# Full-height lo tiles for the second logits matmul of a two-layer hybrid trunk on one Trainium2 core

## The chip, the cores and the metric

The kernel is one program on one core of one Trainium2 chip. Its time is the device time of one launch in microseconds, and of several runs the median is taken. Lower is better. The profile is one execution of the same program, recorded by the hardware profiler: for each engine every instruction with its start and its length.

The engines are named as in the profile: PE is the tensor engine's matmul, PEld its weight load (a matmul needs its stationary operand loaded first), DVE the vector engine, ACT the scalar engine, POOL the GpSimd engine, and SP the queue that issues the DMAs.

## The reference

The reference is an encoder trunk of two layers over 1024 tokens of width 1024. The first layer is a gated DeltaNet mixer, the second (FoX) a softmax attention with a forget gate. Each layer norms its input, mixes it, multiplies by a SiLU gate, projects back and adds to the residual stream. The change is in the attention of the second layer, with 16 heads of 64 elements each:

```
q = rmsnorm(q, qn_w) * 64 ** -0.5
k = rmsnorm(k, kn_w)
cum = cumsum(log_sigmoid(f + f_bias))          # per head, over the tokens
logits[t, s] = q_t . k_s + cum[t] - cum[s]     # for s <= t, else -inf
p = softmax(logits)
o = (p @ v) * silu(z)
y = o @ w_out
```

All of it is in float32. The kernel's products must be more exact than one pass of the tensor engine in its fast float32 form (fp32r) gives, and so operands are split into a hi part (rounded to fp32r) and a lo part (the rest), and products are summed from two or three passes.

## The kernel before, in words

Layer A (the DeltaNet) takes the first two thirds of the program, the FoX layer the rest. Both are written as Python generators, one for each stream of work. A class `Flow` (its functions `step`, `add`, `bank`, `free`) runs the generators by priority against a model of the tensor engine's time, and so writes out by hand the order of all PE instructions. The model prices a matmul by the number of columns that it streams, and for fp32r at least by the columns of its weights (`_cost`); the number of rows is not in it. The order on the other engines is left to the tile framework, which also puts in the waits for tiles and frees a tile's memory when its readers are done.

The FoX layer goes over eight groups `g` of two heads (`j` = 0, 1), and in each over two halves of 512 tokens (`hh`). The streams are:

- `in_proj` projects the tokens to q, k, v and z, three passes for each product (`mm3`). It supplies the matmuls named `mm` in the profile. It is the longest stream, and the others are placed between its matmuls.
- `post` (inside `in_proj`) transposes the normed q and k of one half into tile `tr` and makes the operands of the logits. For a head that lies in rows `own` (0 to 63 for j = 0, 64 to 127 for j = 1), tile `qs[:, j]` holds the hi part of the scaled q in both halves of its 128 rows (ACT, lines 1332 and 1333), tile `ks[:, j]` holds the hi part of k in rows `own` (ACT, line 1347) and its lo part in the other 64 (DVE, line 1348), and tile `ql` holds the lo part of q in rows `own` (DVE, line 1334). `ql` has one plane for both heads, since they lie in different rows.
- `logits` makes, for each of four row tiles of 128 queries (`tt`) and for each block of up to 512 keys (`b`), one PSUM bank `lg` with two or three matmuls: `qs` with all 128 rows of `ks` (hi times hi, plus hi times lo), then `ql` with the 64 rows `own` of `ks` (lo times hi), and in the block on the diagonal a small bf16 matmul of an identity with the mask. Two banks take turns. DVE adds the gate's sums, takes the row minimum (the logits are kept negated) and writes the block to SBUF (line 1422); ACT takes the exponential (line 1430).
- `values` transposes the probabilities (`pt`), splits them on ACT and DVE (`pth`, `ptl`, lines 1465 and 1466) and multiplies with v into `oT`; `fold_out` divides by the row sums and multiplies with the gate.
- After the last group `out_proj_b` projects back. For the last group (`g == NG - 1`) `fold_out` splits its result into `oh` and `ol` in SBUF; `oh` is taken from the ring of `ql` tiles.

For each head and half there are thus 4 row tiles with one block (first half) or two (second half): 16 heads x (4 + 8) = 192 blocks, each with one `ql` matmul. In the first half every block is on the diagonal; in the second half the first block of a row tile is not and has 512 columns.

The tiles of the FoX layer come from two pools. The one on the right side of SBUF is opened after layer A's output projection and lies over the memory of that layer; a tile in it waits for the last users of what lay there.

Of the kernel before, what the change touches and what calls it, by code (L numbers as in the profile page):

```python
# [12 lines left out]
ALU = mybir.AluOpType  # L13
# [81 lines left out]


class Flow:
    """Emits the pieces of several streams in the order in which the tensor engine shall run them."""

    def __init__(self, tc):  # L100
        self.tc = tc
# [70 lines left out]
def tile_trunk(  # L172
# [158 lines left out]
    def acc_bank():  # L331
        return flow.bank("mm", 2, lambda: pmm.tile([P, 512], F32, name="mm", tag="mm", bufs=2))

# [1 line left out]
    sx = ctx.enter_context(ExitStack())  # L335
    px = sx.enter_context(tc.tile_pool(name="px", bufs=1, side="right"))

# [774 lines left out]
            flow.step()  # L1112


# [1 line left out]
    with ExitStack() as sb:  # L1116
        pb = sb.enter_context(tc.tile_pool(name="pb", bufs=1, reuse_waits="tile"))
        psb = sb.enter_context(tc.tile_pool(name="psb", bufs=1, space=PS))
# [95 lines left out]
        fb = bt([P, 16], "fb")  # L1214
        nc.sync.dma_start(fb, f_bias.broadcast_to([P, 16]))
        cum_d = dram.tile([16, S], F32, name="cum_d", tag="cum_d")

        def forget():
            raw = bt([P, KT, 16], "wf_r")
# [55 lines left out]
        def in_proj(u):  # L1275
            g = u["g"]
            while len(bq) < KT:
                bload()
            ws = [bq.pop(0) for _ in range(KT)]
            for hh in range(2):  # L1280
                yield from hold(lambda: done["unit"] >= 4 * g - 4)
                kn = None
                u["v", hh] = v = bt([P, 4, 2, P], "v", 4, F32R)
                for tt in range(4):
                    t = hh * 4 + tt
                    tok = slice(t * P, (t + 1) * P)
                    yield from hold(lambda: done["n2"] > t)
                    ps = yield from acc_bank()
                    for k in range(KT):
                        hi, lo = ws[k]  # L1290
                        mm3(
                            ps[:, 0:384], h2_h[:, k, tok], h2_l[:, k, tok], hi[:, 0:384], lo[:, 0:384],
                            k == 0, k == KT - 1,
                        )
                        if k < KT - 1:
                            yield 0
                    if kn is None:
                        yield from hold(lambda: done["post"] == 2 * g + hh)
                        kn = bt([P, 4, 2 * P], "kn", 1)
                    sq = bt([P, 256], "sq", 1)  # L1300
                    nc.scalar.activation(sq, ps[:, 0:256], AF.Square)
                    ss = bt([P, 4], "ss", 2)
                    nc.vector.tensor_reduce(
                        ss, sq.rearrange("p (n f) -> p n f", f=64), axis=AX.X, op=ALU.add
                    )
                    nc.vector.tensor_scalar(ss, ss, 1.0 / 64, EPS, op0=ALU.mult, op1=ALU.add)  # L1306
                    rs = bt([P, 4], "rs", 2)
                    nc.gpsimd.tensor_tensor(rs, ss, mhalf[:, 0:4], op=ALU.pow)  # L1308
                    vv = ps[:, 256:384].rearrange("p (n f) -> p n f", f=64)
                    nc.scalar.copy(v[:, tt, :, 0:64], vv)  # L1310
                    nc.vector.tensor_tensor(
                        v[:, tt, :, 64:128], vv, v[:, tt, :, 0:64].bitcast(F32), op=ALU.subtract
                    )
                    nc.vector.tensor_tensor(
                        kn[:, tt].rearrange("p (n f) -> p n f", f=64),
                        ps[:, 0:256].rearrange("p (n f) -> p n f", f=64), bc(rs, 2, 64), op=ALU.mult,
                    )
                    flow.free(ps, R_IP)
                    yield 0

                def post(kn=kn, hh=hh):
                    yield from hold(lambda: done["lg"] >= 4 * g - 4 + 3 * hh)
                    yield Y_Q0
                    tr = yield from pst("tr", 1)
                    for tt in range(4):
                        tr_(tr[:, tt * P : (tt + 1) * P], kn[:, tt, 0:P], ident)
                    qs = bt([P, 2, 512], "qs", 3, F32R)
                    ql = bt([P, 512], "ql", 3, F32R)
                    for j in range(2):
                        own, oth = slice(64 * j, 64 * j + 64), slice(64 - 64 * j, 128 - 64 * j)  # L1330
                        sc = qk_c[own, 0:1]
                        nc.scalar.activation(qs[own, j], tr[own], AF.Copy, scale=sc)
                        nc.scalar.activation(qs[oth, j], tr[own], AF.Copy, scale=sc)
                        nc.vector.scalar_tensor_tensor(
                            ql[own], tr[own], sc, qs[own, j].bitcast(F32), op0=ALU.mult, op1=ALU.subtract
                        )
                    flow.free(tr, Y_TB)
                    u["q", hh] = (qs, ql)
                    yield Y_Q1
                    tr = yield from pst("tr", 1)  # L1340
                    for tt in range(4):
                        tr_(tr[:, tt * P : (tt + 1) * P], kn[:, tt, P : 2 * P], ident)
                    ks = bt([P, 2, 512], "ks", 4, F32R)
                    for j in range(2):
                        own, oth = slice(64 * j, 64 * j + 64), slice(64 - 64 * j, 128 - 64 * j)
                        sc = qk_c[own, 1:2]
                        nc.scalar.activation(ks[own, j], tr[own], AF.Copy, scale=sc)
                        nc.vector.scalar_tensor_tensor(
                            ks[oth, j], tr[own], sc, ks[own, j].bitcast(F32), op0=ALU.mult, op1=ALU.subtract
                        )  # L1350
                    flow.free(tr, Y_TB)
                    u["k", hh] = ks
                    done["post"] += 1
                    yield 0

                flow.add(post(), 3)
            zs = [None, None]
            for n in range(KT + ZL):
                for hh in range(2):
                    k = n - ZL * hh  # L1360
                    if not 0 <= k < KT:
                        continue
                    if zs[hh] is None:
                        zs[hh] = yield from acc_bank()
                    tok = slice(hh * HALF, hh * HALF + HALF)
                    hi, lo = (w[:, 384:512] for w in ws[k])
                    mm3(zs[hh], hi, lo, h2_h[:, k, tok], h2_l[:, k, tok], k == 0, k == KT - 1)
                    if hh:
                        bload()
                    if k < KT - 1:  # L1370
                        yield 0
                        continue
                    u["z", hh] = zg = bt([P, 512], "zg", 4)
                    th = bt([P, 512], "wraw", 2)
                    nc.scalar.activation(th, zs[hh], AF.Tanh, scale=0.5)
                    nc.vector.scalar_tensor_tensor(zg, th, 1.0, zs[hh], op0=ALU.add, op1=ALU.mult)
                    flow.free(zs[hh], R_Z)
                    yield 0
# [11 lines left out]
        def logits():  # L1390
            yield from hold(lambda: "fg" in done)
            last, cur = {}, None
            for n, (u, hh, j) in enumerate(units()):
# [3 lines left out]
                if cur != 2 * g + j:  # L1397
# [1 line left out]
                    cumb = bt([P, S], "cumb", 1)  # L1399
                    nc.sync.dma_start(cumb, cum_d[cur : cur + 1, :].broadcast_to([P, S]))  # L1400
                    yield 2500
                hp = slice(64 * j, 64 * j + 64)
                qa, ql = u["q", hh]
                sums = bt([P, 4], "sums", 3)
                pts = []
# [2 lines left out]
                for tt in range(4):  # L1408
# [4 lines left out]
                    for b in range(hh + 1):  # L1413
                        w = min(512, L - b * 512)
                        ka = u["k", b][:, j]
                        ps = yield from pst("lg", 2)
                        last_b = b == hh
                        mm(ps[:, 0:w], qa[:, j, qs], ka[:, 0:w], start=True, stop=False)
                        mm(ps[:, 0:w], ql[hp, qs], ka[hp, 0:w], start=False, stop=not last_b)
                        if last_b:  # L1420
                            mm(ps[:, w - P : w], identb, maskb, start=False, stop=True)
                        nc.vector.tensor_tensor_reduce(  # L1422
                            out=lg[:, b * 512 : b * 512 + w], in0=ps[:, 0:w],
                            in1=cumb[:, b * 512 : b * 512 + w], op0=ALU.add, op1=ALU.min,
                            scale=1.0, scalar=3.0e38 if b == 0 else mx[:, 0:1],
                            accum_out=mx[:, b : b + 1],
                        )
                        flow.free(ps, R_LG)
                        yield Y_G1
# [53 lines left out]
        def fold_out(u, hh, j, sums, og):  # L1483
# [13 lines left out]
                return  # L1497
            if g == NG - 1:
                nc.vector.tensor_tensor(og, og, u["z", hh], op=ALU.mult)
                oh, ol = bt([P, 512], "ql", 3, F32R), bt([P, 512], "zg", 4, F32R)  # L1500
                split(oh, ol, og, lo_eng=nc.vector)
                tail["o7", hh] = oh, ol
                tail["o7t", hh] = flow.t + Y_O7
# [221 lines left out]
```

## Time and profile before

| | before |
|---|---|
| median of 3 runs | 2207.39 us (2204.01 to 2208.75) |
| span of the profiled execution, first to last instruction | 2203.7 us |
| PE busy (matmul) | 1917.6 us, 87% |
| PEld busy (weight load) | 1541.6 us, 70% |
| DVE busy | 1587.4 us, 72% |
| ACT busy | 1048.1 us, 48% |
| POOL busy | 798.0 us, 36% |
| mean granted clock of the tensor engine | 0.940 |
| first and last `ql` matmul | 1478.1 and 2117.2 us |

The page of the profile lists no other time for the profiled execution than its span. A row of the timeline has the start in us, the length in us, the engine, the line, the operation, the tiles as out<-in, for PE the rows*columns of the weights, the shape of the operand, and in brackets the idle time of the engine ahead of it with what ended it ("issue": nothing that the profile shows). Matmuls are pipelined: their lengths overlap, and what a matmul takes of the engine is read from one start to the next. Many lines of code are helpers: L121 is the matmul call of `Flow`, L125 its transposes, L314 the subtraction of `split`, and the tiles tell which work it is.

### The profile page before, as it was taken

What the parts mean: (1) busy time and instruction counts of PE and PEld (TensorE: products, weight loads), DVE (VectorE), ACT (ScalarE), POOL (GpSimd) and SP (SyncE); (2) the same over time, 40 slices, a digit from 0 to 9 for tenths busy, and PEclk for the clock granted to TensorE, in tenths of its full rate; (3) what the DMA queues carried; (4) which work ended last, traced back from release to release, by engine and by line L of the source; (5) the groups of instructions that cost most, each with busy time, mean ns of one, the idle gap of its engine ahead of it and who ended that gap; (6) DMA issues with size and microseconds to landing.
All of it is one profiled execution on the core that took longest, in us unless ns stands there. A gap on an engine that the chain in (4) does not pass through costs nothing.

```text
span 2203.7 us, 32163 instructions
## 1 busy us (share of the span) xinstructions
PE 1917.6 (87%) x10860; PEld 1541.6 (70%) x10860; DVE 1587.4 (72%) x3625; ACT 1048.1 (48%) x2530; POOL 798.0 (36%) x642
## 2 busy tenths in 40 slices
PE   3667888888888888888899779999999999999998
PEld 3555666666667666777777557778888888888776
DVE  8888887888867888788877767546556556566664
ACT  3343444544446455544545445335555455555631
POOL 4343344434445343444423646431221321321212
PEclk7878898999999899999999889999999999999899
DMA  6543333343344232333236676310111111110522
GB/s 243 164 138 118 99 108 103 92 112 108 97 122 123 84 90 90 95 90 88 84 117 215 231 259 229 107 54 25 53 44 39 53 44 39 53 48 26 177 74 93
DMA packets 168088, 232.86 MB, mean 106 GB/s; under 512 B 66858, under 2 KB 107074, under 8 KB 167924
## 3 DMA queue, kind: packets, MB, share of 16 engines
q1 hardware_dynamic: 167924, 230.82, 33.7%
q8 instruction: 85, 1.39, 0.3%
q14 instruction: 79, 0.65, 0.1%
HBM read 203.88 MB, written 26.88 MB: 105 GB/s over the span
## 4 chain that ended last, share of the span: by engine, by line
PE 47%; DVE 28%; DMA 9%; issue 6%; ACT 5%; POOL 3%; SPq 2%; DVEq 0%; POOLq 0%; ACTq 0%
PE mm L121 28%; PE lg L121 8%; DVE xtmp L1009 5%; DVE xi L1013 5%; DVE cv_y L707 4%; PE oT L121 3%; PE pt L125 3%; PE tr L125 2%; DMA oraw<-in_ada_w_dram 2%; DVE ohi L260 1%; DMA oraw<-og_d 1%; PE su L121 1%; ACT whi L311 1%; DMA rmat<-rb 1%; DMA rb<-xi 1%
## 5 line engine op out<-in xcount | busy, mean ns | idle before, releaser
L121 PE MATMUL mm<-ht_h,whi 128*128 128x512 f32 x784 | 358.0, 457 | 6.6 <-DVE olo L287 4.4
L314 POOL TENSOR_TENSOR wlo<-wlo,whi 128x1024 fp32r<-128x1024 f32 x99 | 242.0, 2445 | 327.6 <-issue 176.5
L121 PE MATMUL mm<-ht_l,whi 128*128 128x512 f32 x784 | 321.1, 410 | 6.4 <-DVE ht_l L554 3.8
L121 PE MATMUL mm<-ht_h,wlo 128*128 128x512 f32 x784 | 321.4, 410 | 1.7 <-POOL wlo L314 1.7
L707 DVE SCALAR_TENSOR_TENSOR cv_y<-cv_t,conv_h,cv_y 128x512 f32<-128x512 f32 x192 | 191.6, 1000 | 37.9 <-ACT cv_y L699 36.8
L1009 DVE TENSOR_TENSOR xtmp<-lr,xi 128x60 f32<-128x60 f32 (+24 forms) x496 | 172.4, 348 | 29.6 <-DMA lr<-lb 14.5
L1308 POOL TENSOR_TENSOR rs<-ss,mhalf 128x4 f32<-128x4 f32 x64 | 64.5, 1007 | 355.6 <-DVE ss L1306 352.5
L121 PE MATMUL mm<-whi,h_h 128*128 128x384 f32 x512 | 190.5, 372 | 1.4 <-ACT whi L311 1.4
L121 PEld LDWEIGHTS mm<-ht_h,whi 128*128 128x128 f32 x784 | 156.1, 199 | 38.8 <-DVE olo L287 5.3
L121 PEld LDWEIGHTS mm<-ht_h,wlo 128*128 128x128 f32 x784 | 155.2, 198 | 37.9 <-POOL wlo L314 2.1
L121 PEld LDWEIGHTS mm<-ht_l,whi 128*128 128x128 f32 x784 | 156.4, 199 | 35.4 <-DVE ht_l L554 6.5
L121 PE MATMUL mm<-wlo,h_h 128*128 128x384 f32 x512 | 173.3, 339 | 2.0 <-POOL wlo L314 2.0
L121 PE MATMUL mm<-whi,h_l 128*128 128x384 f32 x512 | 173.0, 338 | 0.0
L311 ACT CAST whi<-wlo 128x1024 fp32r<-128x1024 f32 x100 | 104.7, 1047 | 132.8 <-PE mm L121 62.7
L1466 DVE TENSOR_TENSOR ptl<-pt,pth 128x512 fp32r<-128x512 f32 x192 | 106.1, 555 | 82.1 <-ACT pth L1465 81.1
L1013 DVE TENSOR_TENSOR xi<-xi,xtmp 128x60 f32<-128x60 f32 (+24 forms) x496 | 154.2, 311 | 11.1
L1465 ACT CAST pth<-pt 128x512 fp32r<-128x512 f32 x192 | 91.5, 477 | 141.4 <-PE pt L125 139.6
L1430 ACT ACTIVATE lg<-lg,mx 128x896 f32<-128x896 f32 (+7 forms) x128 | 99.6, 778 | 76.8 <-DVE mx L1422 72.1
L1422 DVE CUSTOM_DVE_ANT_0 lg<-lg,cumb 128x512 f32<-128x512 f32 (+3 forms) x128 | 75.5, 590 | 50.5 <-PE lg L121 49.7
L314 POOL TENSOR_TENSOR wlo<-ht_h,whi 128x1024 fp32r<-128x1024 f32 x31 | 78.6, 2536 | 88.1 <-ACT whi L311 79.3
L711 ACT ACTIVATE cv_t<-cv_y 128x512 f32<-128x512 f32 x64 | 40.3, 630 | 147.3 <-DVE cv_y L707 132.9
L314 DVE TENSOR_TENSOR olo<-oraw,ohi 128x256 fp32r<-128x256 f32 x96 | 79.5, 843 | 37.1 <-ACT ohi L311 36.3
(338 smaller groups left out, 4962.3 us busy)
## 6 DMA issues: line engine op xcount, KB each, us to landing
wlo<-in_wa_c_dram SPq DMA_DIRECT2D x64, 512.0 KB
ht_h<-in_wa_o_dram SPq DMA_DIRECT2D x62, 512.0 KB
oraw<-in_ada_w_dram SPq DMA_DIRECT2D x128, 128.0 KB
wlo<-in_wa_z_dram SPq DMA_DIRECT2D x32, 512.0 KB
gb<-g_d SPq DMA_DIRECT2D x32, 512.0 KB
wraw<-in_wb_dram SPq DMA_DIRECT2D x56, 256.0 KB
oraw<-og_d SPq DMA_DIRECT2D x96, 128.0 KB
cumb<-cum_d SPq DMA_DIRECT2D x18, 512.0 KB
```

What stands on the lines that cost most here:

```text
L121: self.nc.tensor.matmul(out, lhsT, rhs, start=start, stop=stop)
L125: self.nc.tensor.transpose(out, src, ident)
L311: nc.scalar.copy(hi, src)
L314: (lo_eng or nc.gpsimd).tensor_tensor(lo, src, hi.bitcast(F32), op=ALU.subtract)
L707: nc.vector.scalar_tensor_tensor(y, raw[:, j : j + HALF], w[:, j : j + 1], y, op0=ALU.mult, op1=ALU.add)
L1009: (nc.gpsimd if XP else nc.vector).tensor_tensor(tv, bc(lr[:, j + 1 :, j], 1, m), xi[:, 0:m, j : j + 1].broadcast_to([P, m, n]), op=ALU.mult,)
L1013: (nc.gpsimd if XP else nc.vector).tensor_tensor(xi[:, 0:m, j + 1 :], xi[:, 0:m, j + 1 :], tv, op=ALU.subtract)
L1308: nc.gpsimd.tensor_tensor(rs, ss, mhalf[:, 0:4], op=ALU.pow)
L1422: nc.vector.tensor_tensor_reduce(out=lg[:, b * 512 : b * 512 + w], in0=ps[:, 0:w], in1=cumb[:, b * 512 : b * 512 + w], op0=ALU.add, op1=AL ...
L1430: nc.scalar.activation(lg, lg, AF.Exp, scale=-1.0, bias=mx[:, hh : hh + 1], accum_out=sums[:, tt : tt + 1],)
L1465: nc.scalar.copy(ph_[:, cs], pp[:, cs])
L1466: nc.vector.tensor_tensor(pl_[:, cs], pp[:, cs], ph_[:, cs].bitcast(F32), op=ALU.subtract)
```

## The change

The lo part of q moves into three tiles that are made once, `qlz`, with a plane of 128 rows for each head. The half of a plane that is not the head's own is set to zero by POOL at the start of the layer and never written again. `post` takes them in turn and writes rows `own` of plane `j`. The second matmul of a logits block then uses all 128 rows of `ql[:, j]` and of `ks[:, j]`; the rows beside the head's own hold zero times the lo part of k. `oh` of the last group moves from the ring of `ql` to that of `qs`. The tiles take 12 KB of a partition where the ring took 6, and the reserve for DMA descriptors in SBUF is set to 1024 bytes a partition. Two comments and a docstring go.

```diff
@@ in tile_trunk, layer B
         cum_d = dram.tile([16, S], F32, name="cum_d", tag="cum_d")
+        qlz = [bt([P, 2, 512], f"ql{i}", 1, F32R) for i in range(3)]
+        for v in qlz:
+            nc.gpsimd.memset(v[64:P, 0].bitcast(F32), 0.0)
+            nc.gpsimd.memset(v[0:64, 1].bitcast(F32), 0.0)
@@ in post
                     qs = bt([P, 2, 512], "qs", 3, F32R)
-                    ql = bt([P, 512], "ql", 3, F32R)
+                    ql = qlz[(2 * g + hh) % 3]
...
                         nc.vector.scalar_tensor_tensor(
-                            ql[own], tr[own], sc, qs[own, j].bitcast(F32), op0=ALU.mult, op1=ALU.subtract
+                            ql[own, j], tr[own], sc, qs[own, j].bitcast(F32), op0=ALU.mult, op1=ALU.subtract
                         )
@@ in logits
-                hp = slice(64 * j, 64 * j + 64)
                 qa, ql = u["q", hh]
...
                         mm(ps[:, 0:w], qa[:, j, qs], ka[:, 0:w], start=True, stop=False)
-                        mm(ps[:, 0:w], ql[hp, qs], ka[hp, 0:w], start=False, stop=not last_b)
+                        mm(ps[:, 0:w], ql[:, j, qs], ka[:, 0:w], start=False, stop=not last_b)
@@ in fold_out
-                oh, ol = bt([P, 512], "ql", 3, F32R), bt([P, 512], "zg", 4, F32R)
+                oh, ol = bt([P, 512], "qs", 3, F32R), bt([P, 512], "zg", 4, F32R)
@@ in kernel
-    nc = _bacc.Bacc("TRN2", target_bir_lowering=False, num_devices=1)
+    nc = _bacc.Bacc("TRN2", target_bir_lowering=False, num_devices=1, dynamic_dma_scratch_size=1024)
```

## The prediction, on record before the result

> **What bounds the kernel now.** I read the page first: the span, the busy time of the tensor engine and the chain that ended last. The kernel has two layers in a row, and the diff touches only the second, the FoX layer, so the question is who sets the pace there.
>
> ```profile
> span 2203.7 us, 32163 instructions
> PE 1917.6 (87%) x10860; PEld 1541.6 (70%) x10860; DVE 1587.4 (72%) x3625; ACT 1048.1 (48%) x2530; POOL 798.0 (36%) x642
> PE mm L121 28%; PE lg L121 8%; DVE xtmp L1009 5%; DVE xi L1013 5%; DVE cv_y L707 4%; PE oT L121 3%; PE pt L125 3%; PE tr L125 2%; DMA oraw<-in_ada_w_dram 2%; DVE ohi L260 1%; DMA oraw<-og_d 1%; PE su L121 1%; ACT whi L311 1%; DMA rmat<-rb 1%; DMA rb<-xi 1%
> ```
>
> The logits (tile lg) hold 8% of the chain as work of the tensor engine. Next I read busy time by stage (columns: length, PE, weight loads, DVE, ACT, POOL, granted clock, DMA share, GB/s). The first row is the change of layers, the second one of the eight head-pair groups of the FoX layer, the third its last group with the start of the output projection.
>
> ```profile
> 1405.00:1478.00 73.00, 68.31 (x365) 57.24 (x363) 32.76 (x94) 27.52 (x58) 28.07 (x24) 0.98 0.22 71
> 1802.00:1886.00 84.00, 83.83 (x460) 69.34 (x459) 48.36 (x126) 45.47 (x100) 21.53 (x19) 1.00 0.15 46
> 2052.00:2120.00 68.00, 63.90 (x268) 44.73 (x266) 45.90 (x94) 38.50 (x79) 16.24 (x12) 0.87 0.43 141
> ```
>
> In the middle row PE is busy 83.83 of 84 us at full clock, while DVE has 48.36 and ACT 45.47. So PE alone is the bound there. The list of waits, from 1478 to 2120 us, says the same: the largest wait of PE for the evacuation of a logits bank is this, over all 192 pairs of logits matmuls (total, times, longest).
>
> ```profile
> PE lg L121 <- DVE mx L1422: 1.7, 4, 1.2
> ```
>
> But a busy PE is not a PE at its peak. Each logits block is a matmul with the stacked query (qs, all 128 rows) and one with its lo part (ql, 64 rows). The answer for tile ql counts the second kind: 96 with 512 columns and 32 each with 384, 256 and 128.
>
> ```profile
> L121 PEld LDWEIGHTS lg<-ks,ql x192: 182/183/286, 1478.1 to 2117.2; 64*128 64x128 f32 x192
> L121 PE MATMUL lg<-ks,ql x192: 322/490/793, 1478.1 to 2117.2; 64*128 64x512 f32 x96, 64*128 64x128 f32 x32, 64*128 64x256 f32 x32, 64*128 64x384 f32 x32
> ```
>
> The timeline shows what such a matmul costs; read the starts, not the lengths, since matmuls are pipelined. First a pair without a mask:
>
> ```profile
> 1816.15 0.39 PE L121 MATMUL lg<-ks,qs 128*128 128x512 f32 x1
> 1816.46 0.18 PEld L121 LDWEIGHTS lg<-ks,ql 64*128 64x128 f32 x1 [0.30 <-issue]
> 1816.47 0.50 PE L121 MATMUL lg<-ks,ql 64*128 64x512 f32 x1
> 1816.90 0.19 PEld L121 LDWEIGHTS mm<-whi,h_h 128*128 128x128 f32 x1 [0.25 <-issue]
> 1816.90 0.44 PE L121 MATMUL mm<-whi,h_h 128*128 128x384 f32 x1
> 1817.01 0.19 PEld L121 LDWEIGHTS mm<-wlo,h_h 128*128 128x128 f32 x1
> 1817.18 0.34 PE L121 MATMUL mm<-wlo,h_h 128*128 128x384 f32 x1
> 1817.35 0.34 PE L121 MATMUL mm<-whi,h_l 128*128 128x384 f32 x1
> ```
>
> Among full-height matmuls the next weights load while the current matmul runs: the load at 1817.01 stands 0.17 us ahead of its matmul at 1817.18, and that one follows into the next after 0.17 us. At the 64-row matmul this stops twice. Its own load starts only at 1816.46, with its matmul, 0.31 us after qs; and the next full-height load starts only at 1816.90, 0.43 us after ql, again with its matmul, which then holds its successor back to 0.28 us instead of 0.17. Neither waits for any other engine ("issue"). Full-height matmuls into one bank, such as wlo,h_h and whi,h_l in the last two rows, show no such gap, so it is not the shared bank; what is different is the height.
>
> What the pitch is without a change of height is seen here at 256 and 512 columns:
>
> ```profile
> 1807.05 0.28 PE L121 MATMUL oT<-pth,v 128*128 128x256 f32 x1
> 1807.17 0.28 PE L121 MATMUL oT<-ptl,v 128*128 128x256 f32 x1
> 1807.29 0.40 PE L121 MATMUL mm<-h_h,whi 128*128 128x512 f32 x1
> 1807.52 0.39 PE L121 MATMUL mm<-h_l,whi 128*128 128x512 f32 x1
> ```
>
> That is 0.12 us at 256 and 0.23 at 512 columns; for 128 columns I use the 0.12 of 256 as well, an upper end.
>
> **The change part by part.** First, the ql weights and the ks rows become full height in all 192 second matmuls. The count of matmuls, their columns and their order stay: the order is written by a model that prices a matmul by its columns, and no pause between pieces is changed. Unmasked pair (64 of them, the first block of every row tile in the later half of the queries): now 0.32 + 0.43 + 0.28 = 1.03 us from qs to the second matmul behind ql; without the gaps 0.23 + 0.23 + 0.17 = 0.63. That saves 0.40, times 64 is 25.6 us. The other 128 pairs end in a mask matmul. With 512 columns:
>
> ```profile
> 1820.63 0.39 PE L121 MATMUL lg<-ks,qs 128*128 128x512 f32 x1
> 1820.95 0.50 PE L121 MATMUL lg<-ks,ql 64*128 64x512 f32 x1
> 1821.38 0.10 PEld L121 LDWEIGHTS <-identb 128*128 128x128 bf16 x1 [0.25 <-issue]
> 1821.39 0.23 PE L121 MATMUL lg<-maskb,identb 128*128 128x128 bf16 x1
> 1821.43 0.42 PE L121 MATMUL mm<-whi,h_h 128*128 128x384 f32 x1
> 1821.68 0.33 PE L121 MATMUL mm<-wlo,h_h 128*128 128x384 f32 x1
> ```
>
> Here 0.32 + 0.44 becomes 0.23 + 0.23 and saves 0.30. What follows the mask (0.04 + 0.25) I leave as it is: the small mask matmul is too short to hide a weight load, at any height. The narrow ones:
>
> ```profile
> 1812.12 0.22 PE L121 MATMUL lg<-ks,qs 128*128 128x128 f32 x1
> 1812.27 0.33 PE L121 MATMUL lg<-ks,ql 64*128 64x128 f32 x1
> 1812.53 0.23 PE L121 MATMUL lg<-maskb,identb 128*128 128x128 bf16 x1
> ...
> 1814.99 0.28 PE L121 MATMUL lg<-ks,qs 128*128 128x256 f32 x1
> 1815.20 0.38 PE L121 MATMUL lg<-ks,ql 64*128 64x256 f32 x1
> 1815.51 0.23 PE L121 MATMUL lg<-maskb,identb 128*128 128x128 bf16 x1
> ```
>
> At 128 columns 0.15 + 0.26 becomes 0.12 + 0.12 and saves 0.17; at 256, 0.21 + 0.31 becomes 0.24 and saves 0.28; for 384 I take 0.29, between its neighbours. Masked pairs: 32 x (0.30 + 0.29 + 0.28 + 0.17) = 33.3 us. Gross gain: 25.6 + 33.3 = 59 us, all on the path, since PE is the bound.
>
> What that uncovers. The DVE evacuation of each bank, the exponentials and the transposes now have about 0.35 us less cover per pair. One wait per group is nearly due already:
>
> ```profile
> 1813.50 0.50 PE L121 MATMUL lg<-ks,qs 128*128 128x512 f32 x1 [0.17 <-DVE mx L1422]
> ```
>
> Two pairs stand ahead of it (the one at 1812.12 and the one before that), in a stretch whose other end is a weight strip's DMA, which does not come sooner. So about 0.6 us comes back as a wait in each of some seven groups: 4 us. In the last group (third row of the stages) PE already idles 4.1 of 68 us and holds an eighth of the pairs, 7 us of gain; I take 2 us of it as lost there. Bounds for these waits: nothing, as nearly all pairs wait for nothing today, and 15 us, if all of the last group's gain goes and the group wait doubles. I take 6, near the lower end because the measured waits are. DVE would rise from 48.36 of 84 us to 48.36 of about 77, 63%: no new bound.
>
> Second, six memsets on POOL at the start of the layer, and the waits of the three tiles for layer A's memory. Nearest rows, a memset of this width, and the kernel's DMA queue:
>
> ```profile
> L488 POOL MEMSET tmat<- 128x512 f32 x2 | 1.0, 518 | 0.0
> q1 hardware_dynamic: 167924, 230.82, 33.7%
> ```
>
> 6 x 0.52 = 3.1 us on an engine that is busy 28.07 of 73 us in that stage. What stands behind them on POOL are the small powers of the norm and the lo halves of layer B's first operands; PE waits for those. Cost from 0 (they fall in gaps) to 3.1 plus a wait for the old tiles of about as much, 6 us; I take 1, since more than half of POOL's stage is idle. A gain is excluded: nothing is removed from POOL.
>
> [...] SP gets no DMA more or less.
>
> Sum, against the profiled execution: 2203.7 - 59 + 6 + 1 = 2151.7 us of span, a gain of 52. The page gives no other time for that execution than its span; the span lies 3.7 us under the median of the runs, 2207.39. I carry that over: 2155 us.
>
> **The rivals.** (a) *The height is not the cause.* If the gap comes from something else, nothing is gained: 2207 to 2211 with the memsets. For it: the diff only pads with zeros, so PE does the same columns. Against it: 192 late loads, and none between neighbours of equal height. [...]
>
> (b) *The mask keeps its gap.* In this trace the bf16 mask follows nothing but a 64-row matmul, so its late load (1821.38) may come from the change of type. Then each masked pair saves only its first gap, 0.09, 0.09, 0.09 and 0.03 us by width: 32 x 0.30 = 10 us, with 25.6 of the others 35, less 7: 28 us, 2179. Against it: bf16 back to f32 right after the mask runs with only 0.04 us between the starts.
>
> (c) *Stalls drop the clock, and it ends slower.* The tensor engine's clock fell where PE stalled:
>
> ```profile
> 2067.56 0.80 PE L121 MATMUL oT<-pth,v 128*128 128x512 f32 x1 [1.34 <-ACT pth L1465]
> 2071.58 0.79 PE L121 MATMUL lg<-ks,qs 128*128 128x512 f32 x1 [1.19 <-DVE mx L1422]
> ```
>
> There the same 512 columns take 0.80 and 0.79 us instead of 0.40 and 0.39; with a mean clock of 0.87 over 68 us, some 9 us of full-speed work were lost, and the idle time was 4 us. If the shorter pairs made every one of the eight groups stall like that, seven more such events cost 7 x 13 = 91 us against 52: 2246. It decides from four events on. Against it: in the middle group PE idles 0.17 us, and I find 0.6 us more.
>
> **How the numbers follow.** Forecast 0.77, at 2155: its own range runs from 2144 (no waits, and the clock's dip in the last group gone in part) to 2170 (all the waits at their upper bounds). Rival (b) 0.11, (a) 0.06, (c) 0.06. The range 2144 to 2181 holds the forecast and (b), and leaves out the other two and some of the forecast's edges. A difference of 0.2%, 4.4 us, is about what a measurement of this kernel can tell from none. Faster by more than that: 0.77 and 0.11, with a little of the others: 0.89; within it: 0.05; slower: 0.06.
>
> **What would show it.** Right: ql rows read 128*128; their weight loads start with the qs matmul, not with their own; pitch 0.23 us at 512 columns before and behind ql; middle groups near 77 us instead of 84 with PE still without idle time; DVE's share up to about 63%. Rival (b) shows as a mask load that is still late by 0.2 us, (c) as a granted clock under 1.00 in the middle groups, (a) as unchanged gaps. The prediction is wrong if the pairs do shrink but the groups stay at 84 us, which would mean a wait that I did not see.

## The result and the profile after

The changed kernel takes 2158.86 us (median of 4 runs, 2157.18 to 2165.32) against 2208.07 us (median of 4 runs, 2204.01 to 2213.96): a ratio of 0.9776, with a 95% interval from 0.9753 to 0.9799. The forecast was 2155 us, and the gain is 49 us where 52 were forecast. The profiled execution is the slowest of the four, 2165.32 us, of which its span holds 2163.6. The page of the changed kernel begins:

```profile
span 2163.6 us, 32167 instructions
PE 1865.2 (86%) x10860; PEld 1543.0 (71%) x10860; DVE 1586.1 (73%) x3625; ACT 1047.5 (48%) x2530; POOL 800.8 (37%) x648
```

The count of matmuls is the same, 10860, and PE is busy 52 us less; the other engines do what they did, and POOL has its six memsets more. First the pairs themselves, in the timeline of the changed kernel (start, length, engine, line, operation, tiles, rows*columns of the weights, operand). A pair without a mask:

```profile
1790.02 0.40 PE L121 MATMUL lg<-ks,qs 128*128 128x512 f32 x1
1790.02 0.19 PEld L121 LDWEIGHTS lg<-ks,ql 128*128 128x128 f32 x1
1790.25 0.40 PE L121 MATMUL lg<-ks,ql 128*128 128x512 f32 x1
1790.25 0.19 PEld L121 LDWEIGHTS mm<-whi,h_h 128*128 128x128 f32 x1
1790.48 0.34 PE L121 MATMUL mm<-whi,h_h 128*128 128x384 f32 x1
1790.49 0.19 PEld L121 LDWEIGHTS mm<-wlo,h_h 128*128 128x128 f32 x1
1790.66 0.34 PE L121 MATMUL mm<-wlo,h_h 128*128 128x384 f32 x1
```

The load of ql starts with qs at 1790.02, not with its own matmul, and the load behind it starts with ql at 1790.25. From qs to the second matmul behind ql it is 0.64 us, where it was 1.03. And a pair with a mask, 256 columns wide:

```profile
1793.91 0.28 PE L121 MATMUL lg<-ks,qs 128*128 128x256 f32 x1
1794.03 0.28 PE L121 MATMUL lg<-ks,ql 128*128 128x256 f32 x1
1794.15 0.10 PEld L121 LDWEIGHTS <-identb 128*128 128x128 bf16 x1
1794.15 0.23 PE L121 MATMUL lg<-maskb,identb 128*128 128x128 bf16 x1
1794.19 0.42 PE L121 MATMUL mm<-whi,h_h 128*128 128x384 f32 x1
```

Here 0.21 + 0.31 has become 0.12 + 0.12, with the mask's steps behind it as they were: 0.04 us to the next matmul and 0.26 to the one after it, in the median of the 32 pairs of this width, in both kernels. The load of the mask's weights still starts with its own matmul, but the step to that matmul is the plain 0.12 us.

Where the gain is, by stage. The FoX layer's first projection matmul (mm<-whi,h_h) begins in the kernel before at 1402.1 us (this is the row for tile instances in the change of layers, first and last start),

```profile
L121 PE MATMUL mm<-whi,h_h x40: 334/334/422, 1402.1 to 1425.4; 128*128 128x384 f32 x40
```

and in the kernel after at 1408.9 us:

```profile
L121 PE MATMUL mm<-whi,h_h x37: 334/334/423, 1408.9 to 1429.8; 128*128 128x384 f32 x37
```

So in this execution layer A, which the change does not touch, came out 6.8 us longer, and the two spans understate the gain. From that matmul to the end, the FoX stage, it is 2203.7 - 1402.1 = 801.6 us before and 2163.6 - 1408.9 = 754.7 us after: 46.9 us. This stage length proved far steadier than the whole time and is what the experiments below are read by. In the middle group (columns as before) PE is still the bound:

```profile
1805.60:1882.70 77.10, 76.21 (x459) 68.42 (x457) 47.80 (x127) 44.64 (x98) 20.91 (x18) 1.00 0.15 49
```

A group, from its first logits pair to the next group's, is 77.1 us where it was 83.3 (the 84 us in the prediction was the length of its window), at full clock, with 0.9 us of PE idle instead of 0.2. The list of PE's waits in the logits stage, 1484 to 2080 us, tells what filled that (total, times, longest):

```profile
PE lg L121 <- DVE mx L1425: 6.3, 6, 1.3
PE pt L125 <- ACT lg L1433: 3.2, 2, 3.0
PE oT L121 <- DVE ptl L1469: 2.5, 3, 1.1
PE oT L121 <- ACT pth L1468: 1.9, 1, 1.9
PE mm L121 <- POOL wlo L314: 1.5, 3, 0.8
```

With the two smaller rows that the list has besides (1.2 and 0.3 us) that is 16.9 us. In the kernel before, the same list over its own pairs, 1478 to 2120 us, gave 6.0 us. In the FoX layer the order of the instructions in the two traces is the same on all engines up to the last group, but for the six memsets on POOL; so up to there nothing was reordered that could explain the time. In the last group PE's order is the same too, but ACT and DVE take some of their work in another order.

### The profile page after: what moved, and what is told of

Its sections match the earlier page's. It is cut to its first block, busy times and chain, and to the rows that moved or that the text cites. A ratio compares the mean times of both kernels' runs of the same rounds, so it can differ in the third digit from the quotient of the medians.

```text
span 2163.6 us, 32167 instructions
## 1 busy us (share of the span) xinstructions
PE 1865.2 (86%) x10860; PEld 1543.0 (71%) x10860; DVE 1586.1 (73%) x3625; ACT 1047.5 (48%) x2530; POOL 800.8 (37%) x648
## 4 chain that ended last, share of the span: by engine, by line
PE 43%; DVE 30%; DMA 10%; issue 6%; ACT 5%; POOL 3%; SPq 2%; DVEq 0%; POOLq 0%; ACTq 0%
PE mm L121 26%; DVE xtmp L1009 5%; DVE xi L1013 5%; PE lg L121 5%; DVE cv_y L707 4%; PE pt L125 3%; PE oT L121 3%; PE tr L125 2%; POOL wlo L314 2%; DVE ohi L260 2%; DMA oraw<-in_ada_w_dram 2%; DMA wraw<-in_wb_dram 1%; DMA lr<-lb 1%; DMA oraw<-og_d 1%; ACT whi L311 1%
## 5 line engine op out<-in xcount | busy, mean ns | idle before, releaser
L1469 DVE TENSOR_TENSOR ptl<-pt,pth 128x512 fp32r<-128x512 f32 x192 | 106.4, 555 | 84.1 <-ACT pth L1468 82.1
L121 PEld LDWEIGHTS mm<-wlo,h_h 128*128 128x128 f32 x512 | 97.3, 190 | 7.2 <-POOL wlo L314 5.3
```

The lines of the kernel that those rows point to most:

```text
L121: self.nc.tensor.matmul(out, lhsT, rhs, start=start, stop=stop)
L1469: nc.vector.tensor_tensor(pl_[:, cs], pp[:, cs], ph_[:, cs].bitcast(F32), op=ALU.subtract)
```

## The experiments

The theory: across the change from 128 rows to 64 and back PE does not load the next weights ahead (in the kernel before, the loads at 1816.46 and 1816.90 start with their own matmuls), so each 64-row matmul between full-height ones costs a gap on both sides, 0.23 to 0.39 us a pair. Its rivals: the gain is from the new tiles, their place and the smaller reserve; or it is from 64-row matmuls as such; or only one half of the rows is slow. The waits are asked for separately. Every kernel is compared with the kernel before on the same chip; e1 to e4 ran on one chip and e5, e6 and e8 on another. The ratios are taken over all runs of both kernels and can differ a little from the quotient of the medians.

**e1_rows64**, the changed kernel with 64 rows again:

```diff
-                        mm(ps[:, 0:w], ql[:, j, qs], ka[:, 0:w], start=False, stop=not last_b)
+                        hp = slice(64 * j, 64 * j + 64)
+                        mm(ps[:, 0:w], ql[hp, j, qs], ka[hp, 0:w], start=False, stop=not last_b)
```

> The changed kernel with one thing undone: the second logits matmul takes 64 rows of the new full-height planes again. Three tiles with two planes, six memsets, the ring of oh and the smaller descriptor reserve stay. Theory (the change of height between neighbouring matmuls costs about 0.3 to 0.4 us a pair): the time goes back to that of the kernel before, 2208 us within 6, with the late weight loads back (0.32 us from qs to ql at 512 columns). Rival (the gain comes from the new tiles, their place in memory or the reserve): it stays near 2159 us.

Measured: 2212.15 us against 2212.62, ratio 1.0002 (0.9987 to 1.0017). The late loads are back in its timeline:

```profile
1811.92 0.39 PE L121 MATMUL lg<-ks,qs 128*128 128x512 f32 x1
1812.24 0.18 PEld L121 LDWEIGHTS lg<-ks,ql 64*128 64x128 f32 x1 [0.30 <-issue]
1812.24 0.50 PE L121 MATMUL lg<-ks,ql 64*128 64x512 f32 x1
1812.67 0.19 PEld L121 LDWEIGHTS mm<-whi,h_h 128*128 128x128 f32 x1 [0.25 <-issue]
```

The FoX stage is 801.7 us, as before the change. So the height of one matmul holds the whole gain; for tiles, memsets, the ring of oh and the reserve together there is nothing to be seen, within 0.2% in the time and 0.1 us in the stage.

**e2_head0**, full height for the first head of each group alone:

```diff
-                        mm(ps[:, 0:w], ql[:, j, qs], ka[:, 0:w], start=False, stop=not last_b)
+                        hp = (slice(0, P), slice(64, P))[j]
+                        mm(ps[:, 0:w], ql[hp, j, qs], ka[hp, 0:w], start=False, stop=not last_b)
```

> The changed kernel in which only the first head of each group (rows 0 to 63) takes all 128 rows in its second logits matmul; the second head takes 64 rows of its plane. Theory: the price is per pair and does not hang on which half the rows are, so half the gain is left: 2183 us within 6, gaps at the 96 pairs of the second head alone. Rival 1 (any 64-row matmul left in the stage keeps the engine slow for all): near 2208 us. Rival 2 (only one of the two row halves is slow, say 64 to 127): near 2159 or 2208 us.

Measured: 2189.01 us against 2212.62, ratio 0.9901 (0.9865 to 0.9937): a gain of 24 us, about half of the full change's. In the timeline both kinds stand side by side:

```profile
1815.15 0.40 PE L121 MATMUL lg<-ks,qs 128*128 128x512 f32 x1
1815.39 0.39 PE L121 MATMUL lg<-ks,ql 128*128 128x512 f32 x1
...
1827.72 0.40 PE L121 MATMUL lg<-ks,qs 128*128 128x512 f32 x1
1828.05 0.49 PE L121 MATMUL lg<-ks,ql 64*128 64x512 f32 x1
```

0.24 us from qs to ql for the first head and 0.33 for the second. The price is per pair: the middle groups take 80.2 to 81.2 us, midway between 83.3 and 77.1 or up to 1 us above. Nor is it a matter of which rows, since either head's part of the gain is there: this run has the first head's (rows 0 to 63), and the changed kernel has the second head's on top. In the FoX stage, 783.2 us, the gain is 18 of 47 us, less than half; most of what is missing, 3 of 5 us, is in the last group, with 89.3 us from its first pair to the last one where the kernel before has 87.7. PE waits there 4.0 us for ACT at one transpose, a wait that the kernel before does not have and that the changed kernel has with 3.0 us (more on it below).

**e3_split**, the kernel before with the 64-row matmul in two pieces of the same rows:

```diff
-                        mm(ps[:, 0:w], ql[hp, qs], ka[hp, 0:w], start=False, stop=not last_b)
+                        cut = w if w == P else P * (w // P // 2)
+                        flow.t += flow._cost(ql[hp, qs], ka[hp, 0:w])
+                        for c0, c1 in ((0, cut), (cut, w)):
+                            if c1 > c0:
+                                nc.tensor.matmul(ps[:, c0:c1], ql[hp, qs], ka[hp, c0:c1],
+                                                 start=False, stop=not last_b and c1 == w)
```

> The kernel before, with each 64-row logits matmul of 256 or more columns cut into two of the same 64 rows (160 of 192 pairs), one behind the other, with the same weights loaded twice. Theory (the price is for the change of height, not for a 64-row matmul): the second piece's weight load runs under the first piece and follows at its columns' pitch (0.11 to 0.12 us at 256 columns), so each pair grows by at most 0.06 us: 2208 us, at most 2218. Rival (each 64-row matmul has a late load of its own, whatever stands ahead of it): a further gap of 0.1 to 0.2 us in each of 160 pairs, 2224 to 2240 us.

Measured: 2218.16 us against 2212.62, ratio 1.0026 (1.0012 to 1.0039); FoX stage 807.3 us, 5.7 more than before, or 0.04 us for each of the 160 pairs. Its timeline, where two equal neighbours are merged into one row (x2):

```profile
1820.08 0.40 PE L121 MATMUL lg<-ks,qs 128*128 128x512 f32 x1
1820.40 0.30 PEld L1423 LDWEIGHTS lg<-ks,ql 64*128 64x128 f32 x2 [0.37 <-issue]
1820.40 0.50 PE L1423 MATMUL lg<-ks,ql 64*128 64x256 f32 x2
1820.83 0.19 PEld L121 LDWEIGHTS mm<-whi,h_h 128*128 128x128 f32 x1
```

The two pieces take 0.43 us to the next matmul, just what the one 64-row matmul took. A window that begins behind the first piece shows the second by itself, first its weight load and then its matmul:

```profile
1820.51 0.19 PEld L1423 LDWEIGHTS lg<-ks,ql 64*128 64x128 f32 x1
...
1820.63 0.28 PE L1423 MATMUL lg<-ks,ql 64*128 64x256 f32 x1
```

Its load starts 0.12 us ahead of its matmul, under the first piece, as among full-height matmuls. Its matmul follows the first piece after 0.22 us and not after the 0.12 that was expected. I read the difference as the first piece's late load, which holds up what comes behind it; the single 64-row matmul then has it too, as its 0.43 is the same. So a 64-row matmul behind one of its own height adds no gap: it is the change of height that costs, not the height. The narrower pairs, cut into pieces of which at least one has 128 columns, grew by 0.05 us, which is most of the 5.7 us.

**e4_raw3**, the changed kernel with a third raw buffer. It asks for the cause of the new waits. In four groups, the fourth to the seventh, a logits matmul of the changed kernel waits 0.8 to 1.2 us for its bank. The chain of waits shows this detour off PE ahead of it, here in the sixth (start, length, what):

```profile
1863.67 1.30 POOL wlo L314
...
1864.99 2.77 DMA wraw<-in_wb_dram
...
1867.78 0.62 ACT whi L311
...
1868.43 0.69 ACT ks L1351
...
1869.15 0.76 DVE ks L1352
...
1869.94 0.69 DVE lg L1425
```

A strip's DMA waits until POOL has read the raw buffer; ACT's queue stands behind the strip with the ks that the next logits need; DVE stands behind that, and so PE's bank comes late. The edit, at all four places where the tile is taken (one has another shape):

```diff
-bt([P, 512], "wraw", 2)
+bt([P, 512], "wraw", 3)
```

> The changed kernel with three buffers instead of two for the raw weight strips of layer B (tile wraw). It asks what the wait of 0.8 to 1.2 us hangs on that the changed kernel has once a group, where a logits matmul waits for DVE, DVE for ACT, ACT for a strip's DMA, the DMA for POOL. Theory (the strip's DMA, held up by the raw buffer, sets it): the waits go, 0.9 us in each of six groups and some behind weight strips, so 3 to 8 us less than the changed kernel, 2151 to 2156 us. Rival (it is the order of work on ACT and DVE, the buffer does not matter): 2159 us within 3.

Measured: 2160.51 us against 2212.62, ratio 0.9763 (0.9734 to 0.9791). That misses the 2151 to 2156 us that were expected, though the kernel before was 4.5 us slower here than in the first comparison; by the total this kernel could not be told from the change itself. But the FoX stage was 746.9 us against 754.7. That called for a direct comparison, the next two runs.

**e5_after_again** is the changed kernel, unedited.

> The changed kernel as it is, timed beside the two that follow on one chip. It also shows how much of the spread of times lies ahead of the FoX layer: in the runs so far that stage, from the first k/q/v projection to the end, took 754.7 us with the change and 801.5 to 801.8 us with 64 rows, while its start moved between 1398 and 1413 us. Expected: the stage within 2 us of 754.7, whatever the whole time is.

**e6_raw3_again** is the kernel of e4.

> The changed kernel with three raw buffers, once more and beside the changed kernel. In its first run the FoX stage took 746.9 us. Theory (the raw buffer held the strip's DMA, and that the wait of each group): stage at 747 us within 2, groups of 76.0 us, and the whole time 3 to 8 us under the changed kernel's. Rival (the first run was chance): stage back at 755 us, groups of 77 us, no difference.

Measured, with 2209.2 us for the kernel before: e5 2160.19 us, ratio 0.9786 (0.9769 to 0.9802), FoX stage 754.8 us; e6 2152.25 us, ratio 0.9744 (0.9727 to 0.9761), FoX stage 744.6 us. The third buffer is worth 8 us by the medians; the stage of e6 came out 2.4 us under the 747 that were expected. A middle group of e6:

```profile
1722.60:1798.60 76.00, 75.99 (x458) 68.52 (x457) 47.83 (x126) 44.52 (x99) 20.84 (x18) 1.00 0.15 49
```

PE has no idle time left in it, and a group is 83.3 - 76.0 = 7.3 us shorter than before the change, about an eighth of 59.

**e8_rows64_raw3**, both edits (64 rows, three raw buffers):

> Three raw buffers with the 64-row matmul (the changed kernel, both edits). Theory (the waits for the strip are uncovered by the change; before it the tensor engine came too late to meet them): groups stay at 83.2 us and the FoX stage at 799 to 802 us, so nothing worth measuring against the kernel before. Rival (the third buffer is worth 8 us by itself): stage at 794 us.

Measured: 2207.38 us against 2209.2, ratio 0.9997 (0.9982 to 1.0012); FoX stage 799.9 us, groups of 82.9 us. Without the change the third buffer is worth under 2 us in the stage, with it 8 to 10. The waits are thus part of the price of the change, uncovered by the faster pairs. Between the two kernels with three buffers a group differs by 82.9 - 76.0 = 6.9 us.

| kernel | rows of the second matmul | raw buffers | ratio to before | FoX stage, us |
|---|---|---|---|---|
| before | 64 | 2 | 1 | 801.6 |
| e1_rows64 | 64 in new tiles | 2 | 1.0002 | 801.7 |
| e3_split | 64, in two pieces | 2 | 1.0026 | 807.3 |
| e8_rows64_raw3 | 64 in new tiles | 3 | 0.9997 | 799.9 |
| e2_head0 | 128 and 64 | 2 | 0.9901 | 783.2 |
| e5_after_again | 128 | 2 | 0.9786 | 754.8 |
| e4, e6 | 128 | 3 | 0.9763, 0.9744 | 746.9, 744.6 |

The stage is the span less the start of its first projection matmul, which lay between 1398.1 and 1413.0 us.

## Why the prediction was right, point by point

**The gaps go: right.** The middle value of the saving over the pairs was 0.39 us without a mask (forecast 0.40), and with one 0.28 at 512 columns (0.30), 0.28 at 256 (0.28) and 0.23 at 128 (0.17: in 19 of the 32 pairs the pitch from qs to ql fell from 0.15 to 0.06 us, below the bound I had borrowed from 256 columns; in 12 it fell from 0.24 to 0.14, and in one from 0.26 to 0.06). With 0.28 for 384 (forecast 0.29) that is 64 x 0.39 + 32 x 1.07 = 59 us, the forecast's gross gain. e6's groups, which have no waits, give about all of it: 7.3 us each against the kernel before and 6.9 against e8, where an eighth of 59 is 7.4. e1, e2 and e3 show that it is the change of height.

**The waits: right kind, too small.** This is the term that was mis-sized: 6 us forecast, 10.9 measured (16.9 - 6.0). About 5 of them lie ahead of the last group (forecast 4) and nearly 6 in it (forecast 2). The wait of each middle group was forecast at about 0.8 us in all (0.17 + 0.6), and the trace has

```profile
1792.81 0.50 PE L121 MATMUL lg<-ks,qs 128*128 128x512 f32 x1 [0.83 <-DVE mx L1425]
```

It came in four groups and not in seven. What I missed: the last weight strip is late as well in some groups (the wlo row of the list, 1.5 us); with the third buffer that row is gone too. And the last group gained 3.0 us of its 7, from 87.7 to 84.7 us from its first pair to the last one, where I had kept 5. Its waits in the changed kernel begin so:

```profile
2028.47 0.49 PE L121 MATMUL oT<-pth,v 128*128 128x512 f32 x1 [1.89 <-ACT pth L1468]
2030.07 0.80 PE L121 MATMUL oT<-ptl,v 128*128 128x512 f32 x1 [1.11 <-DVE ptl L1469]
2032.48 0.79 PE L121 MATMUL lg<-ks,qs 128*128 128x512 f32 x1 [1.18 <-DVE mx L1425]
...
2046.61 0.47 PE L125 MATMUL pt<-ident,lg 128*128 128x128 f32 x1 [2.98 <-ACT lg L1433]
```

There are few projection matmuls left to place between the pairs. The clock falls there in both kernels (512 columns in 0.80 and 0.79 us), with a mean of 0.90 over these pairs before and 0.94 after. The longest wait, the last row, is again behind a DMA. The chain that ends in it has

```profile
2036.09 4.95 DMA whi<-in_wb_o_dram
...
2041.06 0.62 ACT h_h L311
```

The DMA of this strip of the output weights is issued by a queue that had waited for DVE to read a raw buffer (to 2035.05 us), and in ACT's queue the exponential stands behind the strip. With the third buffer this wait is gone in e4 and in e6, and the last group takes 84.1 and 82.2 us. The other waits of the group stay as they are with three buffers. No experiment was made on them; that ACT and DVE cause them is read from the rows, and as the order of work on these two engines changed in this group as well, it stays open how much of them comes from the faster pairs.

**The memsets: 1 us forecast, none found.** They ran one behind the other on POOL, from 1415.56 to 1418.95 us, 0.52 us each as the nearest row had said (the last one 0.56):

```profile
1415.56 0.52 POOL L1219 MEMSET ql<- 64x512 f32 x1
```

From the first projection matmul to the first logits pair it is 75.5 us with them and 75.8 without: POOL, busy 34.1 of those 75.5 us, hid them in its slack.

**The sum.** 59 - 10.9 = 48 us against 46.9 in the stage; the last 1 us is not assigned. The medians give 49, within the spread that layer A adds.

**The rivals.** That the height is not the cause (a) fell with e1. That the mask keeps its gap (b) fell in the trace: 0.12 us from ql to the mask at 256 columns. That stalls drop the clock in every group (c) did not come: 1.00 in the middle groups. For the height speaks too that in the changed kernel the full-height loads run under full-height matmuls: the load at 1790.25 starts together with ql, 0.23 us ahead of its own matmul.

## What to carry to other kernels

Where PE is the bound, read the starts in its timeline and not its busy share: here a 64-row matmul between full-height ones was brought to 128 rows with zeros in the operand that is written anyway, at no price in columns, and that was worth 0.23 to 0.39 us for each such matmul. Then look for the wait that has almost no slack left and follow it back to its start: here one raw buffer of 2 KB a partition gave back most of what the faster pairs had uncovered (7.8 and 10.2 us of the FoX stage in e4 and e6, of 10.9 us of new waits). And time a change by the stage that it touches, when another stage brings most of the spread.

## What the runs showed of the hardware

In the kernel before, at 512 columns and from start to start (the pair at 1816.15), the step into the lower height took 0.09 us more than the pitch of 0.23, and the step out of it 0.20 more, with another 0.10 at the matmul after that. The weight loads make the two changes look alike: behind each the first load starts with its own matmul, and the next load 0.11 us later (out of the lower height 1816.90 and 1817.01 in the kernel before, into it 1820.40 and 1820.51 in e3). If those 0.11 us are what a late load costs, each change takes about 0.09 + 0.11 us, and two of them the 0.39 us of a pair without a mask. That split is an estimate from these rows; no run separates its two parts. In e3 a 64-row matmul directly behind another of the same rows added neither: its load started 0.12 us ahead of it (1820.51 and 1820.63), and the two together took the 0.43 us of the one.

In the changed kernel a bf16 matmul behind an fp32r one of equal height followed at the plain pitch, 0.12 us at 256 columns and 0.24 at 512, as the forecast had counted on. This is no proof that a change of type is free. The mask's load still starts with its own matmul (both at 1794.15), the steps behind the mask are as long as they were (0.04 us and then, in the median, 0.31 in the pairs of 512 columns and 0.26 in the narrower ones, in both kernels), and at 128 columns the step to the mask took 0.12 us, where ql followed qs in 0.06 in 20 of the 32 pairs. That the mask matmul is too short to hide a weight load, the forecast's reason for the steps behind it, was an estimate; no run separates that from the change of type.
